# Soft-routed mixture of experts on one core: the order of two row pairs and the timing of accumulating and weight transfers

## The chip, the core and the metric

One core of one Trainium2 chip. The metric is device time in microseconds (us), lower is better. PE is TensorE, DVE VectorE, ACT ScalarE, POOL GpSimd and SP SyncE; SP, ACT and POOL also issue DMAs, each in the order of its own program.

## The reference

```python
probs = softmax(router_logits)                       # (16, 512, 8)
for e in range(8):
    output += probs[:, :, e:e+1] * np.matmul(x, expert_weights[e])
# x (16, 512, 512), expert_weights (8, 512, 2048), output (16, 512, 2048), float32
```

Read as one matrix product, the left matrix has 8192 rows and 8 x 512 = 4096 columns (x scaled by each expert's probability), the right one is all weights, 4096 x 2048.

## The kernel before

**Two levels of a seven-product scheme.** Rows are cut in blocks of 256; the blocks 2q and 2q + 1 are row pair q, for q = 0 to 15. With experts 0 to 3 and 4 to 7 as the two halves of the inner dimension and the left and right 1024 columns as halves of the output, a row pair's result is four blocks, C11, C12, C21 and C22, computed from seven products P1 to P7. Each product is split once more in the same way into seven steps of 8 matmuls (`STEPS`, line 353: 1, 5, 6, 2, 7, 3, 4). Some stages go a third level down for their first steps (`by_thirds`). C11 is the sum of P1 and P2, and this is where the adds of this study act.

**Stages.** `stages` lists one or two products each, and `run(k)` issues them in order, step by step. A place in this program is (stage, slot): a slot is one step of one product, a stage of two products has 14, and the planner prices a slot at `SLOT = 1.73` us. The stages by number:

| stage | products | from, us |
|---|---|---|
| 0 to 6 | P1 of row pairs 2 to 15, two a stage (pairs 0 and 1 in the prologue) | 41 to 211 |
| 7 (`ND`) to 14 | P2 of row pairs 0 to 15, two a stage | 211 |
| 15 (`k5`), 16 | P5 of 0 and 1; P6 of 0 | 400 |
| 17 to 30 | P6 of q with P5 of q + 1 | 436 |
| 31 (`k7`) | P6 of 15, P7 of 0 | 778 |
| 32 to 46 | P4 of q with P7 of q + 1 | 802 |
| 47 (`k3`) | P4 of 15, P3 of 14 | 1168 |
| 48 to 55 | P3 of 0 to 13, two a stage; P3 of 15 | 1193 |

Stages 1 to 5, 8 to 13 and 48 to 54 go by thirds. A stage of two products takes about 24.2 us, one by thirds 23.4.

**DVE's order.** DVE makes left operands (x block times probabilities, `Left.make`, `times`), sums of weights and most evacuations. Makes and sums wait in a queue with a cost each (`later`); `slack` lets the queue run in program order as far as a planned clock allows. DVE executes in that order, so an instruction that waits for data holds the evacuations behind it. The left operands of stage s + 1 are queued in the first slots of stage s.

**x blocks** (`XBlock`). The first time, a block of x is cast on POOL into `xs` (`begin`), transposed by two DMA transposes on SP (`finish`, line 415) and stored by SP as a ready block (`store`); later products load that with one SP DMA. `start_loads(s + 2)` is called in the first slots of stage s, `finish_loads(s + 2)` at slot 7. P1 does this for pairs 4 to 15; the blocks of pairs 2 and 3 were built by PE in the prologue and stored; the blocks of pairs 0 and 1 are needed in this form first by P2. All these tiles come from `xpool`, 10 buffers.

**Results.** Every evacuated half block lies in one of 12 buffers of `hpool` (tag `h`) until its DMA has read it: POOL sends it to `out` or, for P1, to `kept` in DRAM. The results of P4 and P3 are sent with an accumulating DMA. `add_kept(q, n, t)` is such a DMA too: 256 KB of `kept[q]`, P1's result, added in DRAM onto C11 in `out`, where P2 stored before. There are 16 x 4 of these, all on POOL, hung into slots by `at`.

**Weights.** `wpool` has 15 buffers of 1 MB. The weight sums of P7 and P4 are made a quarter at a time while P5 and P6 run, in the one buffer left: `by_parts(stage, slot, every, r, load, between, when)` asks on POOL for the four blocks of a quarter (`begin`, which first runs the previous quarter's sums if they are still queued), queues what comes between `when[0]` slots later, and queues the four sums `when[-1]` slots later; each sum is sent on POOL to DRAM. The next quarter starts `every` slots after the last, and its loads wait until the last sends have landed. P7's quarters are loads of 256 KB (`t3`); P4's are three casts of raw weights and one load, less `t2` in between (`less_t2`, which sends `t4`). `turnover` later fetches the finished sums as whole buffers on ACT's queue, 1 MB each, as PE frees those of the product before: P7's in stages 29 to 31, P4's in 30 to 32, P3's in 46 and 47.

`slots_after(stage, slot, n)` gives the place n slots on; line 107 is the helper `tt` of all DVE tensor operations, 118 `sp`, 121 `pool`, 130 `mm`, 164 `fetch_w`; lines 593 to 614 are ACT's and DVE's evacuations.

Of the kernel before, what the change touches and what calls it, by code (L numbers as in the profile page):

```python
# [31 lines left out]
def kernel(  # L32
# [51 lines left out]
    with tc.tile_pool(name="psum0", bufs=1, space=bass.MemoryType.PSUM) as psum0:  # L84
        zero = h_tile([P, NB], f16)
        nc.vector.memset(zero, 0.0)
        every = psum0.tile([P, 8, NB], f32, name="every")
# [32 lines left out]
    def pool(o, i, **how):  # L120
        note(nc.gpsimd.dma_start(out=o, in_=i, **how))  # L121
# [12 lines left out]
    def new_w():  # L134
        return wpool.tile([P, K8, NB], f16, name="w", tag="w")
# [234 lines left out]
    def flush(task):  # L370
        while task is not None and not task.done:
            queue.popleft().run()
# [252 lines left out]
    ND = 7  # L625
# [27 lines left out]
    def at(stage, slot, make):  # L653
        hooks.setdefault((stage, slot), []).append(make)

    def add(*products):
        stages.append(products)
        return len(stages) - 1
# [36 lines left out]
    def product(r, q, **how):  # L695
        left, loads = left_of(r, q)
        lefts[r, q] = left
        p = None
        if r == 1:
            def sink(tn, o):  # L700
                pool(kept_rows(q)(tn), o)
            p = Product(right[1], left, sink)
        elif r == 2:
            p = Product(right[2], left, to_out(q, 0, 0))
        elif r == 5:
            bases[6, q] = m1 = Base(kept_rows(q))
            m1.task = {}

            p = Product(right[5], left, to_out(q, 1, 0))
        elif r == 6:  # L710
            m1 = bases[6, q]

            def base(tn):
                need(m1.task[tn])
                return m1.t[tn]
            p = Product(right[6], left, to_out(q, 0, 1), base)
        elif r == 7:
            base = bases[7, q] = Base(lambda tn: out_rows(q, 0, 1, tn))
            p = Product(right[7], left, to_out(q, 1, 1), base)
        elif r == 4:  # L720
            p = Product(right[4], left, to_out(q, 1, 0, accum_op=ADD), products[7, q].o.__getitem__)
        else:
            p = Product(right[3], left, to_out(q, 0, 1, accum_op=ADD), **how)
        p.loads = loads
        products[r, q] = p
        return p
# [121 lines left out]
    for q in range(2, 16, 2):  # L848
        add(product(1, q), product(1, q + 1))
    xs.clear()  # L850
    for q in range(0, 16, 2):
        add(product(2, q), product(2, q + 1))
    xs.clear()
    k5 = add(product(5, 0), product(5, 1))
# [3 lines left out]
    some = product(6, 15)  # L858
    xs.clear()
    k7 = add(some, product(7, 0))  # L860
    for q in range(15):
        add(product(4, q), product(7, q + 1))
    some = product(4, 15)
    xs.clear()
    k3 = add(some, product(3, KEPT_Z))
# [89 lines left out]
    for i, (kn, e) in enumerate((kn, e) for kn in (ODD, (0, 0), (1, 1), (1, 0)) for e in range(2)):  # L955
        stage = ND + i - 2 if kn != ODD else 2 + 2 * i
# [18 lines left out]
    def sums_in_place(part, b, r, cost):  # L975

        def one(p, o, x, y):
            def make():
                tt(o, x, y, SUB)
                part(p, o)  # L980
            return later(cost, make)
        one(5, b[0, 0], b[0, 1], b[0, 0])
        one(7, b[0, 1], b[1, 1], b[0, 1])
        one(6, b[1, 1], b[1, 1], b[0, 0])
        return one(4, b[1, 0], b[1, 0], b[1, 1])
# [13 lines left out]
    def slots_after(stage, slot, n):  # L999
        slot += n  # L1000
        while slot >= 7 * len(stages[stage]):
            slot -= 7 * len(stages[stage])
            stage += 1
        return stage, slot

    def part_of(what, kn, chunks):
        return kept_w(what, kn)[:, chunks, :]
# [3 lines left out]
    def by_parts(stage, slot, every, r, load, between, when):  # L1011

        for j in range(4):
            b, chunks = {}, ds(2 * j, 2)

            def begin(b=b, j=j, chunks=chunks):
                flush(last_part[0])
                t = new_w()
                for i, kn in enumerate(ORDER):
                    b[kn] = t[:, ds(2 * i, 2), :]  # L1020
                    load(b[kn], kn, j, chunks)

            def go_on(b=b, chunks=chunks):
                for kn in b:
                    if kn != ODD:
                        between(b[kn], kn, chunks)

            def end(b=b, chunks=chunks):
                last_part[0] = sums_in_place(lambda p, o: pool(part_of((r, p), (0, 0), chunks), o), b, r, 0.69)
            at(*slots_after(stage, slot, j * every), begin)  # L1030
            if between is not None:
                at(*slots_after(stage, slot, j * every + when[0]), go_on)
            at(*slots_after(stage, slot, j * every + when[-1]), end)
# [8 lines left out]
    def load_part(what):  # L1042
        def load(t, kn, j, chunks):
            pool(t, part_of(what, kn, chunks))
        return load
# [7 lines left out]
            pool(part_of("t4", kn, chunks), t)  # L1053
        later(0.69, make)

    by_parts(k5 + 2, 4, 13, 7, load_part("t3"), None, (7,))
    by_parts(*slots_after(k5 + 2, 4, 56), 28, 4, load_p4, less_t2, (9, 20))
    by_parts(k7 + 4, 4, 36, 3, load_part("b22"), None, (9,))


# [47 lines left out]
    def add_kept(q, n, t):  # L1108
        pool(out_f[ds(2 * q * HQ + t * HP, HP), ds(n * NB, NB)], kept[q][n, ds(t * HP, HP), :], accum_op=ADD)

    for q in range(16):
        for i in range(4):
            where = (ND + 3, 14 * q + 3 * i) if q < 4 else (k7 + 1, 21 * (q - 4) + 5 * i) if q < 14 else (k3 + 2, 14 * (q - 14) + 3 * i)
            at(*slots_after(where[0], 0, where[1]), lambda q=q, i=i: add_kept(q, i // 2, i % 2))

    finish = products[3, 15]
    finish.base = Base(lambda tn: out_rows(15, 0, 1, tn))
# [81 lines left out]
```

## Time and profile before

| | |
|---|---|
| median of 3 runs | 1374.97 us (1372.62 to 1376.87) |
| the profiled execution | 1376.47 us |
| its span | 1374.7 us, TensorE clock 0.999 granted on the mean |
| DVE, POOL, ACT busy | 82%, 34%, 19% of the span |
| DMA | 365.10 MB, mean 266 GB/s |

A line of the timeline gives start, us, engine, line of the kernel, operation, output<-inputs, shape and count, and in brackets the idle time of that engine before it with what ended it. A line of a table of windows gives from:to, us, then busy us and (instructions) of PE, its weight loads, DVE, ACT and POOL, then granted clock, the share in which the DMA engines were busy, and GB/s. A line of DMA issues gives output<-input, queue, count, KB each and median us from issue to landing. "POOLq" and "SPq" are the issuing side of a DMA.

### The profile page before, as it was taken

How to read it: one execution, taken by the hardware profiler on the slowest of the kernel's cores; microseconds unless marked ns; L12 is line 12 of the kernel's file. 1: busy time of each engine (PE TensorE's matmuls, PEld its weight loads, DVE VectorE, ACT ScalarE, POOL GpSimd, SP SyncE). 2: the span in 40 equal slices, each digit the busy share in tenths (PEclk: the TensorE clock that was granted, in tenths of full speed). 3: DMA queues.
4: the chain of work that ended last, by engine and by line, in shares of the span. 5: the costliest groups of instructions: out<-in, count | busy, mean ns of one | idle time of the engine just before them, and what ended most of it. 6: DMA issues, size and time to landing. Idle time of an engine off the chain costs nothing.

```text
span 1374.7 us, 18740 instructions
## 1 busy us (share of the span) xinstructions
PE 1356.7 (99%) x6822; PEld 664.7 (48%) x6822; DVE 1125.2 (82%) x1369; ACT 263.5 (19%) x525; POOL 461.2 (34%) x707
## 2 busy tenths in 40 slices
PE   9999999999999999999999999999999999999998
PEld 4455545555544444444444444444444444556564
DVE  7876758878878888888987987888989897898884
ACT  3333312333221111111111100000000000224331
POOL 3223313244422334333332133343443433233331
PEclk9999999999999999999999999999999999999999
DMA  9899997899999999999999999999998999999976
GB/s 185 238 218 247 267 253 214 219 269 275 241 326 297 302 312 329 309 310 280 329 264 342 332 380 263 237 233 254 244 263 221 276 229 305 330 298 270 215 127 120
DMA packets 193677, 365.10 MB, mean 266 GB/s; under 512 B 53552, under 2 KB 82480, under 8 KB 188464
## 3 DMA queue, kind: packets, MB, share of 16 engines
q0 software_dynamic: 93536, 199.80, 62.1%
q1 hardware_dynamic: 96304, 137.76, 32.8%
q10 hardware_dynamic: 3744, 26.35, 4.9%
q8 instruction: 53, 0.87, 0.2%
q14 instruction: 40, 0.33, 0.1%
HBM read 215.78 MB, written 186.84 MB: 293 GB/s over the span
## 4 chain that ended last, share of the span: by engine, by line
PE 81%; DMA 15%; issue 2%; DVE 1%; POOL 1%; ACT 0%; DVEq 0%; POOLq 0%; ACTq 0%
PE ps L130 62%; PE pt L130 19%; DMA out_dram<-h 5%; DMA w<-wd 3%; DMA xT<-x 2%; DMA wd<-w 1%; DMA out_dram<-kept 1%; DMA w<-in_expert_weights_dram 1%; DMA xs<-in_x_dram 1%; DMA pT<-p_dram 1%; DMA h<-out_dram 1%; DVE h L107 0%; POOL w L121 0%; DVE z L107 0%; POOL out_dram L121 0%
## 5 line engine op out<-in xcount | busy, mean ns | idle before, releaser
L130 PE MATMUL ps<-w,z 128*128 128x512 f16 (+1 forms) x3768 | 822.8, 375 | 10.0 <-DVE h L107 7.4
L130 PEld LDWEIGHTS <-z 128*128 128x128 f16 x5272 | 516.0, 98 | 592.1 <-issue 14.9
L121 POOL DMA_DIRECT2D out_dram<-h x380 | 253.7, 694 | 639.3 <-ACT h L614 202.5
L130 PE MATMUL pt<-w,z 128*128 128x512 f16 (+1 forms) x1504 | 317.7, 359 | 1.2 <-DMA w<-in_expert_weights_dram 0.8
L107 DVE TENSOR_TENSOR z<-xT,pT 128x2048 f16<-128x2048 f16 x220 | 265.4, 1216 | 14.1 <-DMA xT<-xs 14.1
L107 DVE TENSOR_TENSOR h<-ps,h 128x512 f32<-128x512 f32 x244 | 166.2, 687 | 107.3 <-PE ps L130 87.7
L130 PE MATMUL ps<-w,d 128*128 128x512 f16 x880 | 199.1, 379 | 0.0
L601 ACT COPY h<-ps 128x512 f32<-128x512 f32 x122 | 71.5, 586 | 435.9 <-PE ps L130 353.3
L130 PEld LDWEIGHTS <-d 128*128 128x128 f16 x880 | 86.1, 98 | 100.0
L107 DVE TENSOR_TENSOR z<-z,d 128x2048 f16<-128x2048 f16 x110 | 131.6, 1216 | 0.0
L107 DVE TENSOR_TENSOR w<-w 128x1024 f16<-128x1024 f16 (+2 forms) x117 | 114.2, 990 | 13.8 <-DMA w<-wd 5.8
L107 DVE TENSOR_TENSOR h<-pt,h 128x512 f32<-128x512 f32 x123 | 83.4, 685 | 35.3 <-PE pt L130 34.0
L614 ACT COPY h<-ps 128x512 f32<-128x512 f32 x48 | 28.1, 586 | 377.7 <-PE ps L130 327.0
L107 DVE TENSOR_TENSOR d<-z 128x1024 f16<-128x1024 f16 x110 | 74.2, 684 | 5.3 <-PE ps L130 4.1
L107 DVE TENSOR_TENSOR ps<-ps,h 128x512 f32<-128x512 f32 (+1 forms) x86 | 49.7, 579 | 24.2 <-PE ps L130 20.9
L597 ACT COPY h<-ps 128x512 f32<-128x512 f32 x97 | 53.8, 603 | 81.5 <-PE ps L130 67.0
L121 POOL DMA_DIRECT2D out_dram<-kept x64 | 61.4, 1002 | 17.9 <-DMA out_dram<-h 12.8
L121 POOL DMA_DIRECT2D kept<-h x56 | 30.7, 549 | 104.4 <-ACT h L601 66.2
L593 ACT COPY ps<-ps 128x512 f32<-128x512 f32 x61 | 34.8, 570 | 112.6 <-PE ps L130 70.2
L121 POOL DMA_DIRECT2D wd<-w x77 | 42.6, 555 | 35.4 <-DVE w L107 20.2
L107 DVE TENSOR_TENSOR h<-h 128x512 f32<-128x512 f32 (+2 forms) x69 | 45.0, 674 | 0.1
L107 DVE TENSOR_TENSOR z<-z,u 128x2048 f16<-128x2048 f16 x36 | 44.1, 1224 | 1.2
(73 smaller groups left out, 535.0 us busy)
## 6 DMA issues: line engine op xcount, KB each, us to landing
out_dram<-h POOLq DMA_DIRECT2D x380, 256.0 KB, 7.8
pT<-p_dram SPq DMA_DIRECT2D x126, 256.0 KB, 8.0
w<-wd ACTq DMA_DIRECT2D x25, 1024.0 KB, 10.5
xT<-x SPq DMA_DIRECT2D x80, 256.0 KB, 7.7
h<-out_dram SPq DMA_DIRECT2D x68, 256.0 KB, 5.6
w<-in_expert_weights_dram POOLq DMA_DIRECT2D x33, 512.0 KB, 12.4
out_dram<-kept POOLq DMA_DIRECT2D x64, 256.0 KB, 9.7
h<-kept SPq DMA_DIRECT2D x64, 256.0 KB, 9.1
```

The source lines that it names most:

```text
L107: dve(nc.vector.tensor_tensor(out=o, in0=a, in1=b, op=op))
L121: note(nc.gpsimd.dma_start(out=o, in_=i, **how))
L130: note(nc.tensor.matmul(ps, z, w, start=start, stop=stop, skip_group_check=True))
L593: act(nc.scalar.copy(self.banks["b"], x))
L597: act(nc.scalar.copy(o[tn], q if p == 5 else x))
L601: act(nc.scalar.copy(o[TN[p]], b if p == 2 else x))
L614: act(nc.scalar.copy(o[tn], b))
```

## The change

P2's row pairs 0 and 1 run third (stage 9) instead of first (stage 7); pairs 2 and 3 now run in stage 7, 4 and 5 in stage 8. The quarters of P7's sums start 16 slots apart instead of 13, with their sums queued 10 slots after the request instead of 7. The quarters of P4's start from a place ten slots later and 25 slots apart instead of 28. The adds onto C11: before, pairs 0 to 3 from stage 10, 14 slots a pair; 4 to 13 from stage 32, 21 slots a pair; 14 and 15 from stage 49. After, pairs 2 to 5 from slot 6 of stage 8, 8 slots a pair; 0, 1 and 6 to 13 from stage 34, 18 slots a pair; 14 and 15 from stage 52.

```diff
-    for q in range(0, 16, 2):
+    for q in (2, 4, 0, 6, 8, 10, 12, 14):
         add(product(2, q), product(2, q + 1))
...
-    by_parts(k5 + 2, 4, 13, 7, load_part("t3"), None, (7,))
-    by_parts(*slots_after(k5 + 2, 4, 56), 28, 4, load_p4, less_t2, (9, 20))
+    by_parts(k5 + 2, 4, 16, 7, load_part("t3"), None, (10,))
+    by_parts(*slots_after(k5 + 2, 4, 66), 25, 4, load_p4, less_t2, (9, 20))
     by_parts(k7 + 4, 4, 36, 3, load_part("b22"), None, (9,))
...
-    for q in range(16):
-        for i in range(4):
-            where = (ND + 3, 14 * q + 3 * i) if q < 4 else (k7 + 1, 21 * (q - 4) + 5 * i) if q < 14 else (k3 + 2, 14 * (q - 14) + 3 * i)
-            at(*slots_after(where[0], 0, where[1]), lambda q=q, i=i: add_kept(q, i // 2, i % 2))
+    soon, amid, at_last = (2, 3, 4, 5), (0, 1, 6, 7, 8, 9, 10, 11, 12, 13), (14, 15)
+    for some, stage, slot, every in ((soon, ND + 1, 6, 8), (amid, k7 + 3, 0, 18), (at_last, k3 + 5, 0, 14)):
+        for n, q in enumerate(some):
+            for i in range(4):
+                at(*slots_after(stage, slot, every * n + every * i // 4), lambda q=q, i=i: add_kept(q, i // 2, i % 2))
```

## The prediction, made before the changed kernel was run

> **What bounds the kernel now.** I read the busy table first, then TensorE's (PE's) own timeline for every gap, then what stood behind each gap on DVE, POOL, SP and ACT.
>
> ```profile
> PE 1356.7 (99%) x6822; PEld 664.7 (48%) x6822; DVE 1125.2 (82%) x1369; ACT 263.5 (19%) x525; POOL 461.2 (34%) x707
> ```
>
> PE is busy for 1356.7 of 1374.7 us, so at most 18.0 us of gaps can be won, and nothing that DVE, ACT or POOL save counts unless it closes one. The gaps, from PE's timeline (start, us, what, in brackets the idle time before it and what ended it), with one undisturbed row for comparison:
>
> ```profile
> 205.96 8.75 PE L130 MATMUL ps<-w,z 128*128 128x512 f16 x32 [2.97 <-DVE h L107]
> 221.46 7.07 PE L130 MATMUL ps<-w,z 128*128 128x512 f16 x32
> ...
> 508.58 5.34 PE L130 MATMUL ps<-w,z 128*128 128x512 f16 x24 [1.63 <-DVE h L107]
> ...
> 532.61 7.07 PE L130 MATMUL ps<-w,z 128*128 128x512 f16 x32 [1.43 <-DVE h L107]
> ...
> 800.60 5.35 PE L130 MATMUL ps<-w,z 128*128 128x512 f16 x24 [0.19 <-DMA w<-wd]
> 820.15 3.61 PE L130 MATMUL pt<-w,z 128*128 128x512 f16 x16 [0.38 <-DMA w<-wd]
> 824.62 7.08 PE L130 MATMUL ps<-w,z 128*128 128x512 f16 x32 [0.86 <-DMA w<-wd]
> 845.11 1.89 PE L130 MATMUL ps<-w,z 128*128 128x512 f16 x8 [1.33 <-DVE h L107]
> ...
> 1276.07 1.89 PE L130 MATMUL ps<-w,z 128*128 128x512 f16 x8 [0.58 <-ACT h L597]
> 1278.98 1.24 PE L130 MATMUL ps<-w,z 128*128 128x512 f16 x5 [1.03 <-ACT h L597]
> ```
>
> These gaps sum to 10.40 us; the other 7.6 of the 18.0 lie at the launch and behind the last matmul, which no edit touches. The first gap costs more than its 2.97: the 32 matmuls behind it take 8.75 against 7.07, that is 1.68 more, because the clock fell:
>
> ```profile
> 208.00:210.00 2.00, 2.00 (x6) 0.73 (x5) 2.00 (x2) 0.59 (x1) 1.02 (x2) 0.50 0.86 313
> ```
>
> (the last three columns are the granted clock, the DMA share and GB/s). The gaps of 1.63 and 1.43 show no such loss: 32 matmuls behind the latter take 7.07. So what can be won is 10.40 + 1.68 = 12.08 us, 0.88%, in four places: stage 6 (4.65), stages 19 and 20 (3.06), stages 31 to 33 (2.76), stage 51 (1.61).
>
> **The change part by part.** It adds and removes no instruction: 64 adds onto C11, 30 casts of x, 60 transposes, the same partial sums. Only order and distance move.
>
> *Row pairs 0 and 1 third.* What starved stage 6, in the order POOL, SP, DVE:
>
> ```profile
> 161.77 1.52 POOL L121 DMA_DIRECT2D w<-in_expert_weights_dram  x2 [0.89 <-PE ps L130]
> 163.39 1.42 POOL L121 DMA_DIRECT2D xs<-in_x_dram  x2
> ...
> 178.73 8.59 SPq L415 DMA_TRANSPOSE xT<-xs  x4
> ...
> 192.43 1.23 DVE L107 TENSOR_TENSOR z<-xT,pT 128x2048 f16<-128x2048 f16 x1 [10.56 <-DMA xT<-xs]
> ...
> 198.50 6.81 DVE L107 TENSOR_TENSOR w<-w 128x4096 f16<-128x4096 f16 x3
> ```
>
> Row pairs 0 and 1 are the only ones of P2 whose x was never transposed. The two casts stand behind two weight casts, their data lets SP begin the transposes only at 178.73, and the left operands of stage 7 wait 10.56 us on DVE. DVE then runs its delayed work in program order, 6.81 us of weight sums among it, ahead of the evacuation that PE needs at 203. Pairs 2 and 3 in that place need only plain loads: their x blocks were built in the prologue and stored early. The wait goes, DVE has its 10.56 us back, and the 2.97 and 1.68 go: **-4.65 us**. What is late next is the same work for pairs 0 and 1, now for stage 9. Two casts on POOL come in stage 7, behind the stores of stage 6 and ahead of the two weight casts at 212.71; four transposes and two loads of probabilities on SP, ahead of the loads of stage 10; and two stores of x on SP. Their consumers:
>
> ```profile
> 212.71 1.53 POOL L121 DMA_DIRECT2D w<-in_expert_weights_dram  x2
> ...
> 239.04 0.87 DVE L107 TENSOR_TENSOR ps<-pt,h 128x256 f32<-128x256 f32 x2 [1.60 <-PE pt L130]
> ...
> 241.49 2.35 DVE L107 TENSOR_TENSOR z<-xT,pT 128x2048 f16<-128x2048 f16 x2
> ```
>
> The first left operands of stage 9 are made at 241.49. From 163.39 to 192.43 the chain took 29.0 us behind two weight casts; casts issued by 212.7 with the same 29.0 would be ready at 241.7. So even this worst row costs 0.2 us of DVE's time, and DVE idles 1.60 us just before, at 239, anyway; without weight casts ahead it is earlier. I take 0; the other end is the old gap again, +4.65.
>
> *Sums of P7's quarters three slots later, parts 16 apart instead of 13.* The two gaps at 508 and 532:
>
> ```profile
> 497.73 2.14 POOL L121 DMA_DIRECT2D w<-wd  x4 [7.30 <-DMA wd<-w]
> ...
> 506.28 0.69 DVE L107 TENSOR_TENSOR w<-w 128x1024 f16<-128x1024 f16 x1 [5.51 <-DMA out_dram<-h]
> ...
> 530.54 1.42 DVE L107 TENSOR_TENSOR w<-w 128x1024 f16<-128x1024 f16 x2 [4.16 <-DMA w<-wd]
> ...
> w<-wd POOLq DMA_DIRECT2D x4, 256.0 KB, 8.1
> ```
>
> POOL asks for a quarter only when the previous one's results have landed (7.30 us of waiting), and the loads issued from 497.73 take 8.1 us to land, so that DVE reaches the sums 5.51 and 4.16 us before the data (the first wait is put down to a store that landed at the same time). The evacuations queue behind, and PE stands for 1.63 and 1.43. Three slots of 1.73 us (the planner's SLOT; a quarter of the 7.07 row is 1.77) are 5.19 us: 0.32 and 0 remain. From the sums to the next request there are six slots before and after (13 - 7, 16 - 10), so POOL's wait does not grow. **-3.06 us**; other end 0.
>
> *P4's quarters 25 apart instead of 28, first one ten slots later.* Here cover is given up: from the sums (+20) to the next request five slots instead of eight, and from P7's last sums to the first request eight instead of ten.
>
> ```profile
> 593.25 0.73 POOL L121 DMA_DIRECT2D w<-in_expert_weights_dram  x1 [5.83 <-DMA wd<-w]
> ...
> 594.54 1.43 POOL L121 DMA_DIRECT2D w<-in_expert_weights_dram  x2
> ...
> 608.86 1.28 DVE L107 TENSOR_TENSOR w<-w 128x1024 f16<-128x1024 f16 x2
> ...
> w<-in_expert_weights_dram POOLq DMA_DIRECT2D x3, 256.0 KB, 7.7
> ```
>
> POOL reaches the request 5.19 us sooner, but the landing it waits for does not move: the wait becomes about 5.83 + 5.19 = 11.0 us, with up to a handful of result stores and one cast of x queued behind it. The four loads land where they did, the last near 594.54 + 0.73 + 7.7 = 603.0, while DVE's first subtraction moves from 608.86 to 603.7: 0.7 us of cover is left of 5.9. I take +0.3 us over the three parts; the other ends are 0 and, if each part starves DVE like the quarters of P7 did, 3 x 1.63 = +4.9.
>
> *Adds onto C11 (64 accumulating transfers of 256 KB).* Forty of them ran from stage 32 on, eight in stages 49 and 50; now none runs in stages 32, 33, 49 and 50.
>
> ```profile
> 804.05 1.77 POOL L121 DMA_DIRECT2D out_dram<-kept  x2
> ...
> 832.11 0.69 DVE L107 TENSOR_TENSOR h<-ps,h 128x512 f32<-128x512 f32 x1 [4.87 <-DMA h<-out_dram]
> ...
> 802.00:826.00 24.00, 22.76 (x106) 10.08 (x105) 19.83 (x23) 1.17 (x2) 7.56 (x10) 1.00 1.04 359
> ```
>
> At 802 to 826 the DMA engines are full (share 1.04) with P4's weights and stored rows, and the gaps at 820, 824 and 845 wait for a weight, a weight, and (by the 4.87 us on DVE) a stored row. The two adds at 804.05 stand ahead of these. The first gap (0.19 at 800) is before any add and stays. Of 0.38 + 0.86 + 1.33 = 2.57 I take **-2.0**; the ends are 0 and -2.57.
>
> ```profile
> 1263.15 0.83 POOL L121 DMA_DIRECT2D out_dram<-kept  x1 [0.43 <-DMA out_dram<-h]
> ...
> 1275.43 0.59 ACT L597 COPY h<-ps 128x512 f32<-128x512 f32 x1 [4.88 <-DMA out_dram<-h]
> ...
> 1216.50:1240.00 23.50, 23.50 (x139) 13.41 (x138) 21.48 (x27) 8.35 (x19) 8.21 (x10) 1.00 1.09 287
> 1310.00:1334.00 24.00, 24.00 (x141) 13.57 (x140) 20.43 (x25) 8.28 (x19) 7.18 (x9) 1.00 0.70 92
> ```
>
> In stages 49 and 50 the share is 1.09, result stores land late, and after the last add at 1263.15 ACT waits 4.88 us for a buffer that a store still reads; this is the gap of 0.58 + 1.03. The eight adds move to stages 52 and 53. Stage 53 has room (0.70); the first four, in stage 52, meet the last loads of kept left operands. They end about 30 us before the end. I take **-1.2** of 1.61; the other end is 0.
>
> The sixteen early adds, for pairs 2 to 5, run at seven a stage instead of four, from stage 8:
>
> ```profile
> 258.70:282.00 23.30, 23.30 (x137) 13.24 (x136) 18.43 (x24) 8.23 (x18) 6.80 (x12) 1.00 0.87 245
> ...
> 305.40:328.80 23.40, 23.40 (x138) 13.29 (x137) 18.71 (x24) 8.23 (x18) 11.23 (x18) 1.00 1.07 285
> ```
>
> Four adds raised the share of a stage from 0.87 to 1.07 with no gap on PE, so seven make an estimated 0.87 + 7 x 0.05 = 1.22 in stage 9, for one stage. I take +0.3; the ends are 0 and the 1.61 of stage 51, the nearest row in which stores fell behind.
>
> **Sum**: -4.65 - 3.06 + 0.3 - 2.0 - 1.2 + 0.3 = -10.3 us. The profiled run took 1376.47 with a span of 1374.7, 1.8 around it; 1376.47 - 10.3 = 1366.2. The median, 1374.97, is 1.5 below the profiled run, and 1374.97 - 10.3 = 1364.7. I take 1365.
>
> The clock term can be priced another way. The Trainium skill, "TensorE: Matmul & The Clock Gate", Part 1: The HAM clock gate, has the clock fall only after an idle window of about 3.4 us. By that rule 2.97 us of idling would cost no clock, and the sum would be -8.6. The trace disagrees with it (0.50 at 208 to 210), and the measurement decides.
>
> **The rivals.** *Load moved, not removed.* The bytes are the same and the DMA engines run at 1.0 and above over most of the span; the adds, seven a stage early and four in 18 slots instead of 21 later, make new gaps where they now run, and pairs 0 and 1 a part of the old one. Then only part remains, say 4.65 + 3.06 less 1.61 twice: 4.5 us, 1370.5. For it, the share in stage 52; against it, the 309 us of stages 34 to 46, with adds at a share of 0.98 and PE busy throughout:
>
> ```profile
> 851.00:1160.00 309.00, 309.00 (x1433) 140.04 (x1432) 271.68 (x324) 15.24 (x26) 122.51 (x170) 1.00 0.98 250
> ...
> 1287.00:1310.00 23.00, 23.00 (x136) 13.17 (x135) 19.44 (x25) 8.18 (x18) 7.41 (x9) 1.00 1.02 202
> ```
>
> The Trainium skill, "DMA: Bandwidth & Descriptors", Issuing engines are not separate DMA queues, speaks for this rival: transfers from every queue share the same 16 engines.
>
> *It does not do what it says*: stage 9's transposes come as late as stage 7's did, and P4's quarters give back what P7's win. -4.65 + 4.65 - 3.06 + 4.9 - 3.2 = -1.4: 1373.6.
>
> *Slower.* POOL's wait ahead of P4's quarters. Result stores stand behind it, and there are twelve h buffers. The waits of 5.83 and 7.30 us on landings passed without ACT holding PE; it decides where the stores queued during about 11 us use up the buffers. Uncovered, three parts cost the added 5.19 each, and each such gap the clock's 1.68: 20.6 us, less the 10.6 won elsewhere: +10.0, 1385.0. Against it: a stage of 24 us posts eight results, so about four come due in 11 us.
>
> **How the numbers follow.** Chances: forecast (gain 6.5 to 12) 0.66, load moved 0.20, nothing 0.06, slower 0.08. The forecast's own range is 1362.9 (all 12.08) to 1368.5. Runs of the unchanged kernel lie 2 us about their median, so 1362 below; above, the range takes in most of the first rival, to 1371.5. About 0.3%, 4.1 us, is what a measurement of this kernel can tell from no change; under 1370.9 lie the forecast and about three quarters of the first rival: faster 0.81, same 0.11, slower 0.08.
>
> **What the profile after would show.** Right: no DVE wait on xT before 205 and a clock of 1.00 there; DVE waits under 1 us before the sums of P7's quarters; no PE gap from 815 to 850 and from 1270 to 1285; POOL waits near 9 to 11 us ahead of P4's quarters without a gap on PE. Wrong: a DVE wait on xT near 237; ACT waiting for stores between 235 and 310; DVE waiting on weights between 550 and 730; gaps of PE in stages 52 to 54.

## The result and the profile after

| | median us (executions) | range us |
|---|---|---|
| before | 1373.85 (20) | 1366.96 to 1376.87 |
| changed | 1382.51 (20) | 1375.55 to 1390.67 |

The ratio is 1.0063 (95% interval 1.0043 to 1.0084): about 9 us slower, where 10 us faster was forecast. The executions spread over 15 us where those of before spread over 10, and the mean granted clock goes from 0.998 in one of 1375.61 us to 0.993 in one of 1389.33 us. By an estimate from these clocks, lost clock makes (0.998 - 0.993) x 1388, about 7 of the 14 us between the two; one of 1385.34 us has 0.998, so the clock is not all. The profiled execution is that of 1375.61 us (span 1373.9). It is one of the shortest, and even 0.9 us shorter than the profiled one of the kernel before. So its trace shows where the gaps moved; the 7 us between it and the median are in no trace.

Every gap that the prediction named is gone from it, but for a wait on a weight where stage 32 begins, which grew from 0.19 to 2.03 us. These are PE's gaps now, from its timeline as before:

```profile
281.60 0.62 PE L130 MATMUL ps<-w,h 128*128 128x256 f16 x4 [2.74 <-ACT h L794]
308.11 0.60 PE L130 MATMUL ps<-w,h 128*128 128x256 f16 x4 [1.31 <-ACT h L794]
572.34 3.61 PE L130 MATMUL ps<-w,z 128*128 128x512 f16 x16 [1.00 <-DVE h L107]
599.88 5.08 PE L130 MATMUL ps<-w,z 128*128 128x512 f16 x16 [3.21 <-DVE h L107]
805.56 5.35 PE L130 MATMUL ps<-w,z 128*128 128x512 f16 x24 [2.03 <-DMA w<-wd]
```

They sum to 10.29 us, as much as the old ones (10.40). Windows of the same trace (granted clock, DMA share and GB/s last) show the old place healed and two new ones losing clock:

```profile
203.00:206.00 3.00, 3.00 (x15) 1.36 (x14) 3.00 (x3) 0.81 (x2) 1.08 (x2) 1.00 0.38 145
281.60:284.00 2.40, 2.40 (x14) 1.80 (x14) 0.00 (x0) 0.87 (x3) 2.36 (x4) 0.59 1.07 327
600.00:602.00 2.00, 2.00 (x6) 0.63 (x5) 1.97 (x3) 0.00 (x0) 0.00 (x0) 0.50 1.02 408
1263.00:1287.00 24.00, 24.00 (x141) 13.57 (x140) 21.14 (x26) 8.50 (x19) 7.94 (x11) 1.00 0.98 237
```

PE was idle at 203 to 206; now it is full, and stage 51 (1263 to 1287) is full too. The new gaps lie in stages 9 and 10, at the early adds, and in stages 22 and 23, at the weight quarters. For stages 9 and 10, ACT's timeline shows it waiting for a store that still reads its buffer, which the prediction had named as a sign of being wrong:

```profile
281.18 0.37 ACT L794 COPY h<-ps 128x256 f32<-128x256 f32 x1 [3.18 <-DMA out_dram<-h]
...
307.69 0.37 ACT L794 COPY h<-ps 128x256 f32<-128x256 f32 x1 [1.75 <-DMA out_dram<-h]
```

For the quarters, the chain is read from POOL, SP and DVE of the same trace:

```profile
538.37 2.13 POOL L121 DMA_DIRECT2D w<-wd  x4 [9.71 <-DMA wd<-w]
...
544.95 0.71 POOL L121 DMA_DIRECT2D xs<-in_x_dram  x1 [2.31 <-DMA w<-wd]
...
562.63 0.71 POOL L121 DMA_DIRECT2D w<-in_expert_weights_dram  x1 [3.65 <-DMA wd<-w]
...
566.21 0.75 POOL L121 DMA_DIRECT2D xs<-in_x_dram  x1
```
```profile
582.09 2.64 SPq L415 DMA_TRANSPOSE xT<-xs  x2
584.82 0.81 SPq L118 DMA_DIRECT2D h<-kept  x1
...
588.54 2.76 SPq L118 DMA_DIRECT2D h<-kept  x2
```
```profile
595.54 0.69 DVE L107 TENSOR_TENSOR h<-h 128x512 f32<-128x512 f32 x1 [5.29 <-DMA h<-kept]
```

POOL waits 9.71 us for landings ahead of P7's last quarter, and 3.65 us ahead of P4's first. That one now stands at slot 0, so the cast of x goes out behind it and three weight casts, at 566.21. SP waits for this cast until 582.09, in order, and the kept rows that P6 needs are asked for behind the transposes, at 584.82 and 588.54. DVE waits 5.29 us for them with PE's evacuations behind it, and PE stands for 3.21.

### The profile page after: what moved, and what is told of

It is laid out like the page before. It is cut to its first block, busy times and chain, and to the rows that moved or that the text cites. A ratio compares the mean times of both kernels' runs of the same rounds, so it can differ in the third digit from the quotient of the medians.

```text
span 1373.9 us, 18727 instructions
## 1 busy us (share of the span) xinstructions
PE 1357.3 (99%) x6822; PEld 665.7 (48%) x6822; DVE 1127.4 (82%) x1369; ACT 262.7 (19%) x525; POOL 460.7 (34%) x707
## 4 chain that ended last, share of the span: by engine, by line
PE 77%; DMA 13%; issue 7%; POOL 3%; DVE 0%; ACT 0%; POOLq 0%; DVEq 0%; ACTq 0%; SPq 0%
PE ps L130 59%; PE pt L130 18%; DMA out_dram<-h 4%; DMA wd<-w 4%; DMA w<-in_expert_weights_dram 2%; POOL out_dram L121 2%; DMA w<-wd 1%; DMA xs<-in_x_dram 1%; DMA h<-out_dram 1%; POOL wd L121 0%; POOL w L121 0%; DVE h L107 0%; POOL xs L121 0%; POOLq L121 0%; ACT h L601 0%
## 5 line engine op out<-in xcount | busy, mean ns | idle before, releaser
L121 POOL DMA_DIRECT2D w<-in_expert_weights_dram x47 | 35.5, 774 | 31.6 <-DMA wd<-w 26.7
```

## The experiments

The main theory after this reading: two causes, the seven adds a stage in stages 8 to 10, and a cast of x that leaves late because POOL waits ahead of it. The rivals: one of them alone; the new order of the pairs; P4's sums ending later; or the places that moved later adds fill.

Kernels of one group ran side by side, with the kernel before; differences between groups are taken from the ratios, whose intervals are about 2 to 3 us to either side. Where a diff shows only a tuple or a call, the rest of its line is left out and is as it was.

| group | run | median us | before us | ratio to before (95%) |
|---|---|---|---|---|
| 1 | e1_early_adds_back | 1371.32 | 1372.34 | 0.9996 (0.9977 to 1.0015) |
| 1 | e2_p4_quarters_28 | 1375.24 | 1372.34 | 1.0019 (0.9996 to 1.0043) |
| 1 | e3_both_back | 1368.11 | 1372.34 | 0.9972 (0.9950 to 0.9993) |
| 1 | e4_order_alone | 1368.12 | 1372.34 | 0.9974 (0.9960 to 0.9988) |
| 2 | e5_quarters_as_before | 1364.96 | 1372.74 | 0.9931 (0.9907 to 0.9955) |
| 2 | e6_p7_at_slot_4 | 1368.94 | 1372.74 | 0.9967 (0.9949 to 0.9985) |
| 2 | e8_p7_back | 1374.43 | 1372.74 | 1.0007 (0.9988 to 1.0026) |
| 2 | e7_changed_again | 1376.02 | 1372.74 | 1.0018 (0.9994 to 1.0042) |
| 3 | e9_early_slow | 1363.76 | 1372.22 | 0.9938 (0.9915 to 0.9962) |
| 3 | e10_early_dense | 1373.11 | 1372.22 | 1.0006 (0.9988 to 1.0023) |
| 3 | e11_early_dense_plain | 1363.83 | 1372.22 | 0.9940 (0.9917 to 0.9963) |
| 3 | e12_p7_at_slot_4_p4_later | 1366.86 | 1372.22 | 0.9957 (0.9939 to 0.9974) |
| 4 | e13_p7_changed_alone | 1365.28 | 1373.30 | 0.9947 (0.9928 to 0.9966) |
| 4 | e14_p4_changed_alone | 1367.00 | 1373.30 | 0.9959 (0.9939 to 0.9978) |
| 4 | e15_p7_three_slots_sooner | 1364.11 | 1373.30 | 0.9931 (0.9912 to 0.9950) |
| 4 | e16_p4_late_alone | 1365.06 | 1373.30 | 0.9938 (0.9917 to 0.9959) |
| 5 | e17_both_quarters | 1371.25 | 1371.36 | 1.0010 (0.9990 to 1.0030) |
| 5 | e18_both_p7_sooner | 1366.57 | 1371.36 | 0.9966 (0.9945 to 0.9987) |

**e1** (from the changed kernel)

```diff
-(soon, ND + 1, 6, 8)
+(soon, ND + 3, 0, 14)
```

> The changed kernel, with the adds of pairs 2 to 5 from stage 10 on again, 14 slots a pair, as before. Theory (two causes: seven adds a stage in stages 8 to 10, and P4's first request ahead of a cast of x): the gaps at 281 and 308 (2.74 and 1.31 us, with 1.7 us of lost clock) go, those at 572, 600 and 805 stay; median 5 to 7 us under the changed kernel's 1382.5, about 1376. Rival A (only P4's quarters matter): no change, 1382. Rival B (the new order of the row pairs itself does it): the gaps near 281 and 308 stay.

The gaps near 281 and 308 are gone and a gap of 3.34 us at 593 stays. Those at 572 and 805, which were to stay, are gone too, and one of 4.01 at 761 is new. The ratio falls below that of the result (1.0063), though not clearly below that of the changed kernel in group 2 (e7, 1.0018). Rivals A and B fall for the first two gaps.

**e2** (from the changed kernel)

```diff
-by_parts(*slots_after(k5 + 2, 4, 66), 25, 4, load_p4, less_t2, (9, 20))
+by_parts(*slots_after(k5 + 2, 4, 70), 28, 4, load_p4, less_t2, (9, 20))
```

> The changed kernel, with P4's quarters 28 slots apart again, each asked for at slot 4 of a stage, behind that stage's cast of x; the first four slots later than in the changed kernel. Theory: the gaps at 572 and 600 (1.00 and 3.21 us, with about 1.6 us of lost clock) go, those at 281 and 308 stay; about 1376. Rival A (only P4's quarters matter): under 1370, the old gaps being gone too. Rival C (P7's wider spacing does it): the gaps at 572 and 600 stay.

About the time expected, but not by the way expected: a gap of 2.67 us stays at 574 while the one at 600 goes, so P7's wider spacing has a part in it (rival C). A gap of 1.77 at 820 is new.

**e3** has both diffs.

> Both of these at once: new order of pairs, P7's quarters 16 apart, adds of stage 32 and later moved, early adds and P4's quarters as before. Theory: none of the new gaps but the one at 805 and none of the old ones; the sum of what the prediction named, 1364 to 1368. Rival D (the time lies in the later adds or in the weight fetch near 805): 1373 or more.

The early gaps are gone, 3.62 us stays at 569 and 1.58 at 799. The theory missed P7's part. Against e2, side by side, the early adds as before are worth 7.1 us (1375.24 - 1368.11).

**e4** (from the kernel before)

```diff
-for q in range(0, 16, 2):
+for q in (2, 4, 0, 6, 8, 10, 12, 14):
     add(product(2, q), product(2, q + 1))
```

> The kernel before, with row pairs 0 and 1 of P2 third and nothing else. Theory: the gap at 203 to 206 and its lost clock go, 4.65 us, and all other gaps stay: 1369 against 1373.9. Rival B (the order does the harm): 1378 or more, with a gap near 236 or 281.

As expected: 4.2 us faster, and no gap between 100 and 524 us. Rival B falls.

**e5** (from the changed kernel: e1's diff and)

```diff
-by_parts(k5 + 2, 4, 16, 7, load_part("t3"), None, (10,))
-by_parts(*slots_after(k5 + 2, 4, 66), 25, 4, load_p4, less_t2, (9, 20))
+by_parts(k5 + 2, 4, 13, 7, load_part("t3"), None, (7,))
+by_parts(*slots_after(k5 + 2, 4, 56), 28, 4, load_p4, less_t2, (9, 20))
```

> New order of pairs and the adds of stage 32 and later moved; P7's and P4's quarters and the early adds as before. Theory now (the quarters at slots 6 to 10 and 0 put a cast of x behind POOL's wait; SP's transposes and the loads of kept rows behind them come late): the gap of 3.62 us near 569 with its clock goes, one or two gaps of under 1 us remain near 500 to 530, and those of stages 31 to 33 and 51 are gone; 1363 to 1365. Rival D (the moved later adds give nothing): like the order alone, 1368.

As expected: gaps of 1.08, 1.31 and 0.45 us only. The moved later adds give what separates e5 from e4: about 5.9 us by the ratios (0.9931 and 0.9974), 3.6 by the medians against the kernel before. The traces have e4's gaps from 793 us on summing to 4.30 and e5's to 0.45. Rival D falls. This is faster than both kernels.

**e6** (from e5)

```diff
-by_parts(k5 + 2, 4, 13, 7, load_part("t3"), None, (7,))
+by_parts(k5 + 2, 4, 14, 7, load_part("t3"), None, (8,))
```

> As e5, but P7's quarters 14 apart, so that each is asked for at slot 4 of a stage, three slots behind its cast of x, with the sums 8 slots later instead of 7. Theory: no cast waits behind a quarter, so no gap of 3 us near 570; DVE waits less before the sums than in the kernel before; 1362 to 1365, not slower than e5. Rival E (any wider spacing of P7's quarters makes the gap): 1367 or more with a gap of about 3.6 near 545 to 570.

Wrong. A gap of 4.29 us at 564, but another one: POOL waits 11.20 us ahead of P4's first request, now six slots behind P7's last sums instead of ten, and P4's weights are late for DVE, which waits 4.33 us for them at 562.56 (and 4.63 just before, put down to no wait that the profile shows). So the wait has a second way to PE, through the quarter's own data.

**e8** (from the changed kernel)

```diff
-by_parts(k5 + 2, 4, 16, 7, load_part("t3"), None, (10,))
+by_parts(k5 + 2, 4, 13, 7, load_part("t3"), None, (7,))
```

> The changed kernel with only P7's quarters as before (13 apart, sums 7 later). Theory: the early adds' gaps near 281 and 308 stay (about 6 us with the clock) and P4's first request, now further behind P7's last sums, no longer waits for them; the gaps near 572 and 600 shrink; 1374 to 1378. Rival E: as far down as without any of the quarters' changes, below 1374.

As expected in time; the gaps of 3.30 and 0.97 near 282 and 310 stay, none near 572 or 600, but P7's old gap (3.43 at 535) is back.

**e7** is the changed kernel again.

> The changed kernel once more, unaltered, for a second profile: the first showed one of its fastest executions (1375.61 of a median of 1382.5). Theory: the same places as before (stages 8 to 10, 21 to 23), with larger gaps and more lost clock. Rival F (a slower place that the first profile did not show at all): gaps elsewhere.

The same places: 2.50 and 1.87 near 281 and 308, 1.23 and 2.64 near 573 and 600. Gaps of 1.22 at 676 and 0.90 at 699 are new (rival F, in part), with smaller ones at 772, 781 and 806. The gaps are hardly larger than in the first profile, and this execution too (1376.24) is well below the result's median, so the question of the slower ones stays open. Side by side with e5 it is 11 us slower. Its ratio, 1.0018, is below the 1.0063 of the result, and the intervals barely miss each other.

**e9, e10, e11** (from e5)

```diff
 e9:
-(soon, ND + 3, 0, 14)
+(soon, ND + 1, 6, 14)
 e10:
-(soon, ND + 3, 0, 14)
+(soon, ND + 1, 6, 8)
 e11, besides e10's:
-kept[q][n, ds(t * HP, HP), :], accum_op=ADD)
+kept[q][n, ds(t * HP, HP), :], **({} if q in (2, 3, 4, 5) else {"accum_op": ADD}))
```

> e5 (quarters as before, new order, later adds moved), with the adds of pairs 2 to 5 from stage 8 but 14 slots a pair: the place of the change, the rate of before. Theory (rate): four adds a stage are covered in any of these stages; no gap near 281 and 308; 1364 to 1366 as e5. Rival H (place: stages 8 to 10 have no room): gaps of ACT near 281 or 308 of 1 us or more, 1368 or more.

> e5 with the early adds exactly as changed: from stage 8, 8 slots a pair. Theory (rate): the gaps near 281 and 308 come back, about 4 us with 1.7 us of lost clock in a fast execution and more in others; 1370 to 1373. Rival A (early adds alone are harmless): 1365.

> e10, but the sixteen early transfers write C11 of pairs 2 to 5 instead of adding onto it, so the sum of P1 and P2 is left out there. Same slots, same 256 KB, same order on POOL. Theory (what fills the DMA engines is the reading and writing back of an accumulating transfer): gaps under half of e10's, 1365 to 1368. Rival I (it is the sixteen instructions on POOL and their waits, or the bytes of P1's result alone): as e10.

In time, all three about as the theory has it (e9 and e11 a little under their ranges). The place costs nothing that the intervals show (e9 against e5). The rate costs 9.35 us (e10 less e9), and the same sixteen transfers as plain writes cost nothing at that rate (e11 less e9: 0.07). Not all of the 9.35 is explained. In e10's trace the early gaps sum to 3.95 us, with about 1.6 of lost clock (0.50 for 2.2 us, then 0.76 for 2.0); gaps of 2.49, 1.25 and 1.70 lie at 760 to 804, where nothing was changed between e9 and e10:

```profile
281.81 1.01 PE L130 MATMUL ps<-w,h 128*128 128x256 f16 x4 [2.79 <-ACT h L794]
308.03 0.60 PE L130 MATMUL ps<-w,h 128*128 128x256 f16 x4 [1.16 <-ACT h L794]
760.46 3.61 PE L130 MATMUL ps<-w,d 128*128 128x512 f16 x16 [2.49 <-DVE ps L107]
803.79 5.35 PE L130 MATMUL ps<-w,z 128*128 128x512 f16 x24 [1.70 <-DMA w<-wd]
```

The windows of 254 to 280 us, of e9, e10 and e11 in that order:

```profile
254.00:280.00 26.00, 26.00 (x162) 15.68 (x160) 19.83 (x25) 10.28 (x24) 11.72 (x19) 1.00 1.10 280
```
```profile
254.00:280.00 26.00, 25.01 (x151) 14.60 (x150) 18.47 (x24) 8.94 (x21) 11.76 (x17) 1.00 1.12 270
```
```profile
254.00:280.00 26.00, 26.00 (x163) 15.65 (x161) 19.55 (x24) 10.07 (x23) 11.79 (x22) 1.00 1.08 314
```

The DMA share hardly tells them apart (1.10, 1.12, 1.08), and GB/s set only e11 apart (280, 270, 314). Of the issues from 232 to 300, these are the rows for the stores and the adds, in e9, e10 and e11 (KB each, then median us from issue to landing):

```profile
out_dram<-h POOLq DMA_DIRECT2D x23, 256.0 KB, 8.6
out_dram<-kept POOLq DMA_DIRECT2D x10, 256.0 KB, 10.8
```
```profile
out_dram<-h POOLq DMA_DIRECT2D x20, 256.0 KB, 8.6
out_dram<-kept POOLq DMA_DIRECT2D x16, 256.0 KB, 12.8
```
```profile
out_dram<-h POOLq DMA_DIRECT2D x24, 256.0 KB, 7.2
out_dram<-kept POOLq DMA_DIRECT2D x16, 256.0 KB, 8.4
```

At the same rate an accumulating transfer lands after 12.8 us and a plain one of the same size after 8.4. The stores, once issued, land no later in e10 than in e9 (8.6 in both). What differs is when they are issued: from 270 to 280 us POOL issues five stores in e9 and in e11, but three in e10 and in the changed kernel, and between them it stands for landings. In e10:

```profile
275.56 0.54 POOL L121 DMA_DIRECT2D out_dram<-h  x1 [4.14 <-DMA w<-in_expert_weights_dram]
277.26 0.88 POOL L121 DMA_DIRECT2D out_dram<-kept  x1 [1.17 <-DMA out_dram<-kept]
278.93 0.56 POOL L121 DMA_DIRECT2D out_dram<-h  x1 [0.78 <-DMA out_dram<-kept]
```

From 240 to 310 POOL's waits for landings sum to 21.1 us in e10 and to 10.0 in e9 and in e11. The largest of e10 and then of e9 (what POOL was to write, what it waited for, us in total, times, longest):

```profile
POOL out_dram L121 <- DMA w<-in_expert_weights_dram: 9.2, 3, 4.1
POOL out_dram L121 <- DMA out_dram<-kept: 8.0, 7, 1.5
```
```profile
POOL w L121 <- DMA out_dram<-h: 3.1, 3, 1.5
POOL out_dram L121 <- DMA out_dram<-h: 2.6, 3, 1.3
```

So results stay longer in the twelve h buffers, and of these three traces only e10's has ACT waiting for stores at the gaps. Why a store waits for the landing of other data is not shown. Nor does e11 separate the transfer from its issue: an add takes POOL about 0.9 us to issue in e9 and e10, and about 0.55 in e11.

**e12** (from e3: P7's quarters at slot 4 of each stage)

```diff
-by_parts(k5 + 2, 4, 16, 7, load_part("t3"), None, (10,))
+by_parts(k5 + 2, 4, 14, 7, load_part("t3"), None, (8,))
```

> e3 (both undone), but P7's quarters each at slot 4 of a stage (14 apart, sums 8 later) instead of slots 4, 6, 8 and 10; six slots from sums to the next request in both, P4's quarters the same. Theory (a cast of x behind POOL's wait): the gap of 3.62 us near 569 goes; 1363 to 1366 against e3's 1368. Rival G (the wait itself, wherever it stands): the gap stays, 1367 to 1369.

The gap near 569 is gone, as expected, but the profiled execution has others of 0.57 to 2.59 us from 735 to 819, and the ratio's interval overlaps e3's: inconclusive. It is the longest of its twelve executions (1372.75).

**e13 to e16** (from e9)

```diff
 e13:
-by_parts(k5 + 2, 4, 13, 7, load_part("t3"), None, (7,))
-by_parts(*slots_after(k5 + 2, 4, 56), 28, 4, load_p4, less_t2, (9, 20))
+by_parts(k5 + 2, 4, 16, 7, load_part("t3"), None, (10,))
+by_parts(*slots_after(k5 + 2, 4, 70), 28, 4, load_p4, less_t2, (9, 20))
 e14: only by_parts(*slots_after(k5 + 2, 4, 66), 25, 4, load_p4, less_t2, (9, 20))
 e15: as e13, but by_parts(k5 + 2, 1, 16, 7, load_part("t3"), None, (10,))
 e16: only e13's second line
```

> e9 with P7's quarters as changed (from slot 4, 16 apart, sums 10 later) and P4's from slot 4 of stage 22, 28 apart. Theory (cast of x behind POOL's wait, which falls into slots 10 to 15 of stage 20): DVE waits 4 us or more for kept rows near 560 and PE has a gap of about 3.5 us with lost clock; 1367 to 1369. Rival J (only P4's later end costs): no gap near 565, but gaps near 735 to 820; as e16.

> e9 with P4's quarters as changed (from slot 0 of stage 22, 25 apart), P7's as before. Theory: the first request stands ahead of the cast of x of its stage, but twenty slots behind P7's last sums, so that POOL does not wait there; the next ones (slots 11, 8 and 5) wait about 10 us for landings, the one at slot 11 across the next stage's cast; one gap of 1 to 3 us near 585 to 640; 1365 to 1368. Rival K (five slots from sums to request are too few, wherever they stand): gaps at all three, 1368 to 1372.

> e13 with P7's quarters from slot 1 instead of slot 4 of stage 17: requests at slots 1, 3, 5 and 7, same spacing, same sums 10 slots later, P4 the same. Theory (cast behind the wait): casts of x leave on time, DVE waits under 2 us for kept rows, no gap of 3 us near 565; 2 to 5 us under e13. Rival G (the wait itself): POOL waits as long and the gap stays; as e13.

> e9 with P4's quarters fourteen slots later (from slot 4 of stage 22, 28 apart), P7's as before: the price of P4's later end alone. Theory: up to 1 us, 1364 to 1365. Rival J: gaps near 735 to 820 that are not in e9; 1366 to 1368, as e13.

Alone, each costs little: e13 0.2 us over e16, less than expected, and e14 1.9; the intervals of all three overlap, so neither is clear of noise. The profiled execution of e13 (the longest of its twelve, 1374.57) has the expected gaps, 2.33 and 1.73 us at 568 and 594 behind DVE waits of 5.22 and 3.56 us for kept rows; e15 has none of them and no DVE wait for kept rows, at a median 1.2 us lower, less than expected. e14's gaps are not where they were expected but at 756 to 801. Its trace has none above 0.1 us from 525 to 755, though POOL waits 7.17, 8.08 and 8.64 us ahead of P4's later requests: a wait of that length does not by itself open a gap. e16 shows that P4's later end costs nothing by itself.

**e17, e18** (from e9)

```diff
 e17:
-by_parts(k5 + 2, 4, 13, 7, load_part("t3"), None, (7,))
-by_parts(*slots_after(k5 + 2, 4, 56), 28, 4, load_p4, less_t2, (9, 20))
+by_parts(k5 + 2, 4, 16, 7, load_part("t3"), None, (10,))
+by_parts(*slots_after(k5 + 2, 4, 66), 25, 4, load_p4, less_t2, (9, 20))
 e18: the same with by_parts(k5 + 2, 1, 16, 7, load_part("t3"), None, (10,))
```

> e9 with both P7's and P4's quarters as changed. Theory (they act together: a request of P4 that waits, ahead of a cast of x, after a cast that was already late): gaps near 565 to 600 of 3 us or more in all, with lost clock; ratio to the kernel before 0.998 to 1.000, 1370 to 1373. Rival L (the two only add up, 1 + 3 us): 0.996 to 0.997, 1367 to 1369.

> e17 with P7's quarters from slot 1 instead of slot 4 of stage 17. Theory: P7's waits pass no cast of x and P4's first request no longer waits 4 us or more for P7's last sums; no gap above 1 us near 565 to 600; ratio 0.993 to 0.996, 1364 to 1368 (what is left of P4's part). Rival M (P4's five slots do it all): as e17.

Together they cost what neither costs alone: e17's ratio is 1.0010, against 0.9947 and 0.9959 for e13 and e14, and the intervals do not meet. Three slots for P7 take 4.7 us of that back (e18). PE's gap in e17 and the casts of x, first of e17, then of e18:

```profile
596.32 5.30 PE L130 MATMUL ps<-w,z 128*128 128x512 f16 x16 [5.11 <-DVE h L107]
```
```profile
534.99 2.13 POOL L121 DMA_DIRECT2D w<-wd  x4 [10.80 <-DMA wd<-w]
541.50 0.71 POOL L121 DMA_DIRECT2D xs<-in_x_dram  x1 [2.25 <-DMA w<-wd]
...
563.93 0.75 POOL L121 DMA_DIRECT2D xs<-in_x_dram  x1
```
```profile
526.70 2.13 POOL L121 DMA_DIRECT2D w<-wd  x4 [5.15 <-issue]
...
534.98 0.71 POOL L121 DMA_DIRECT2D xs<-in_x_dram  x1
...
560.60 0.75 POOL L121 DMA_DIRECT2D xs<-in_x_dram  x1
```

In e18 the casts leave 6.5 and 3.3 us sooner, SP's next transposes begin at 569.91 instead of 577.67, and DVE never waits for kept rows there; in e17 it waits 5.25 us for them at 591.98. POOL's wait ahead of P4's first request is nearly the same in both (3.32 and 3.05 us); in e18 POOL comes to it 3 us sooner. Nor is the late start of the cast all: from the second cast to the transposes pass 13.74 us in e17 and 15.88 in the changed kernel, but 9.31 in e18 and 10.95 in e9. What makes the cast itself take longer is not shown.

e17 and e18 also have a gap of 1.78 and 1.16 us near 327 that e9 does not have, behind a wait of ACT for a store (2.22 and 1.60 us). The early adds are those of e9, four a stage, so that rate has little to spare.

## Why the prediction was wrong, step by step

**Row pairs 0 and 1 third: right.** -4.65 forecast, -4.2 measured by the medians (e4 against before), and the late end, stage 9's transposes, never appeared.

**The moved later adds: right.** -3.2 forecast; -3.6 by the medians and -5.9 by the ratios between e4 and e5. The two runs belong to different groups, so the size is rough; the traces' gaps have 3.85.

**The sixteen early adds: the step that failed first.** The prediction took +0.3 with an upper end of 1.61; e10 against e9 gives +9.35, and e2 against e3 +7.1. About 5.5 us of it are seen at the two early gaps in e10's trace; its gaps of 5.44 us in all at 760 to 804 are not explained. The prediction worked from the DMA share, 0.87 + 7 x 0.05, and held the 1.22 that came out for harmless for one stage. The share measured at seven adds is 1.12, hardly more than the 1.10 at four: near 1.1 it no longer shows what the extra adds do. They show in POOL's waits for landings (21.1 us against 10.0), which hold back the stores, until the twelve h buffers are used up and ACT waits. The end of 1.61 also left out the clock, which fell to 0.59 behind a gap of 2.74 us. The first rival named the place and priced each such gap at 1.61.

**P7's quarters: the old gaps closed, a new one opened.** DVE's waits at the sums went, as forecast. "POOL's wait does not grow" failed: it stood for 9.71 us ahead of the last quarter, against 4.94 before (ahead of the second and third for 7.63 and 8.25, against 7.91 and 7.30). And its place was not looked at: the last request moved from slot 1 to slot 10, so the wait now runs into the next stage, over its cast of x. In e15 the requests keep their new spacing but come three slots sooner, no cast is held up behind the wait, and there is no such gap.

**P4's quarters: +0.3 forecast.** The prediction named the cast behind POOL's wait and then priced only the quarter's own data. What it missed is the next queue: SP waits for that cast in order, and behind it stand the kept rows that PE's evacuations need within the stage. Alone the change measures 1.9 us (e14 over e16), not clear of noise, and e14's trace shows no gap from this chain; with P7's change, e17 is about 10 us over e9 by ratio (1.0010 - 0.9938 = 0.0072). In e17's trace 6.8 of these are the gap of 5.11 us at 596 and its lost clock (5.30 against 3.61 us), 1.78 the gap near 327. The prediction added the two edits; they act on one chain. The waits ahead of P4's quarters were 3.65 us for the first and 7.08 to 8.23 for the others, below the 11.0 that it reckoned with.

**The rival "slower" came near in number by another way.** It gave 1385.0, from stores queued behind POOL's wait ahead of P4's quarters until ACT holds PE there. The trace has no gap behind ACT at the quarters; ACT holds PE at the early adds.

The sum of what was measured apart is -4.2 - 5.9 + 9.35 + 9.9 = +9.2 us, against 8.7 (1382.51 - 1373.85). That this is so close is partly luck: each term is uncertain by about 2 us or more, some go by medians and some by ratios, and group 2 has the same changed kernel only 3.3 us over the kernel before (1376.02 - 1372.74).

The clock term held up: 1.68 us forecast behind such a gap, 1.47 measured behind the 3.21 at 600 (5.08 against 3.61) and 1.69 in e17. The Trainium skill's "TensorE: Matmul & The Clock Gate", Part 1: The HAM clock gate, speaks of an idle window of about 3.4 us; the traces do not bear that out as a threshold on the length of one gap, since e15 loses clock after a gap of 2.24 and e14 loses none after one of 3.83:

```profile
1151.59 2.93 PE L130 MATMUL ps<-w,z 128*128 128x512 f16 x8 [2.24 <-DVE h L107]
```
```profile
755.80 3.61 PE L130 MATMUL ps<-w,d 128*128 128x512 f16 x16 [3.83 <-DVE ps L107]
```

Eight matmuls take 2.93 us in e15, against 1.89 in the undisturbed case at 845 before; sixteen take an unhurt 3.61 in e14, and in e2 after the 2.67 us at 574. The length of the gap alone does not decide it.

**Open.** Several kernels (the changed one, e1, e2, e3, e10, e12, e13, e14, e18) show gaps of up to 4 us between 735 and 826, where P7's and P4's weights are fetched; e5, e6, e8, e9, e11 and e16 show under 0.5 there. e9 and e10 differ only near 235 to 310, so this is not a matter of the quarters alone, and e8 has the dense early adds without it. The profiled executions of e12 and e13 are the longest of their kernels, and those of e1, e3, e10, e14 and e18 lie above their medians (those of the changed kernel and e2 below), so it may come and go from one execution to the next; one profile of each does not say what decides it. What makes the result's slower executions slow (1382 and more) is in no trace. Why the result's ratio (1.0063) lies above e7's is not settled either.

## What to carry to other kernels

A request that waits on an in-order queue is priced by everything behind it, then by what waits for that on the next queue, down to the first thing that the critical engine needs; here that was a cast on POOL, a transpose on SP and a row load that DVE needed. Where the DMA engines are near full, judge extra transfers by how long the issuing queue stands for landings and by how many stores still leave, not by the busy share or the median landing of a store, and count an accumulating transfer as clearly more than a plain one. Two edits that each use up the slack of the same chain are tried together before they are added. The best version measured (e5 or e15, ratio 0.9931, intervals 0.9907 to 0.9955 and 0.9912 to 0.9950; e9 and e16 are no different by their intervals) keeps the new order and the moved later adds, and four early adds a stage or fewer.

## What the runs showed of the hardware

Sixteen accumulating transfers of 256 KB in some 32 slots instead of 56 cost this kernel 9.35 us (e10 less e9); as plain writes in 32 slots they cost 0.07 (e11 less e9). At that rate an accumulating one landed after 12.8 us on the median, a plain one after 8.4, with the DMA share at 1.12 and 1.08. POOL took about 0.9 us to issue the one and 0.55 to issue the other. The granted clock fell behind gaps of 2.24 us and more in some executions (0.64 from 1151.6 to 1154 in e15, 0.50 at 600 in the changed kernel) and not behind all of them (1.00 from 756 to 762 in e14, behind 3.83 us).
